# Moving a background task along the kernel, and PSUM copies to ScalarE for a while

## The chip, the cores and the metric

The kernel runs on one core of one Trainium2 chip. The metric is device time in microseconds of one execution; the median of three runs is 2852.82 us (2850.33 to 2859.31).

## The reference

One layer of a hybrid decoder, for a prompt of 2048 tokens and, beside it, 8 sequences of 4 new tokens each ("sample", 32 rows) that attend to caches of 2048 tokens. All is float32, the model width is 1024.

```python
h = rms_norm(x, norm_pre_mix)
q, k, v, z1, z2, g_a, g_b = project_inputs(h, w_in, b_gate)   # one matmul 1024 x 5376, gelu on z, sigmoid on g
for gi, (win, dil) in enumerate(((128, 1), (512, 4), (2048, 16))):   # three head groups, dilated windows
    o, lse = dilated_group_prompt(...)  or  dilated_group_sample(..., cache)
o_a = merge_dilations(outs, lses)                 # weighted by softmax of the lse
o_b = z1 * (tril(w_spatial) @ layer_norm(z2) + b) # gMLP, chunks of 128 tokens
merged = g_a * (o_a @ w_ao) + g_b * (o_b @ w_bo)
x = x + rms_norm(merged @ w_out, norm_post_mix)
f = square(relu(rms_norm(x, norm_pre_ffn) @ w_up)) @ w_down   # 1024 -> 4096 -> 1024
x = x + rms_norm(f, norm_post_ffn)
```

The outputs are the prompt's and the sample's rows, the new keys and values of each group, and the sample's normalised gate rows.

## The kernel before

**Spans.** The prompt is worked in two spans of 1024 tokens; the 32 sample rows ride with span 0, whose rows count 1056. Every matmul operand is split into a high and a low float32r part (`split`, `split_w`, `in_parts`: a cast on ScalarE, then a subtraction on VectorE or GpSimd), and a product takes three matmuls. `gemm` (matmuls at L323) adds them up in a PSUM bank of 512 columns.

**Stages.** For each span: projections of q, k and v with attention behind them (`project`, `attention`: two pairs of heads times three groups), then the gMLP (`gmlp`), then the gates and the merge. In span 0 that is `mix(0)`, eight blocks m of gates, o_a @ w_ao and o_b @ w_bo; in span 1 it is `mix_seven`, which takes the gates of m = 1 to 7 by Strassen's scheme: seven products of quarter matrices (L1236) instead of eight. `out_rows` multiplies by w_out, norms and adds. Then `ffn`: `up(0)` and `down(0)` for span 0, `up(1)` and `down_rows` for span 1, all by the same seven products (matmuls at L1599 and L1707), each over 16 blocks u in `up`. In `up(0)` a product is 4 x 3 x 2 matmuls of 264 columns.

**Weight sums.** The seven products need sums of the quarters of a weight matrix beside the quarters: S1 to S4, for the gates (`gate_sums`), for w_up (`up_sums`) and for w_down (`down_sums`). `weight_sums` makes them in DRAM by DMAs alone, in 20 groups: 4 for the gates, 8 for w_up, 8 for w_down. For each of a group's four sums a plain copy of 512 KB goes out on SyncE's queue (L1454), and one group later an accumulating DMA on GpSimd's queue (L1459) adds the second term. Each of these 160 DMAs is one step of a generator. S2 of a group waits for its S1, S4 for its S2.

**Lanes.** Four deques of generators (`lanes`) hold work that is woven into the main program. `step(lane)` runs the next piece of the first generator in a lane; `tick` steps lanes 0 to 2 at set places inside a product. Lane 0 has attention, gMLP and norm pieces, lane 1 merges and staging, lane 2 sample attention (`sample_attention(0)` and `(1)`, whose VectorE products read the caches piece by piece), one block of the gMLP's gate, `sample_branch` and the next span's first norms (`pre_mix_behind`). Lane 3 has only the weight sums.

**The pacer.** Lane 3 is stepped by columns. `pace(columns)` is called at the start of each `gemm` with the number of k blocks times the columns, and at each of the 49 products of `mix_seven` with 4 x 512:

```python
calls = [-200000]
def pace(columns):
    calls[0] += columns
    if calls[0] > SUM_EVERY:
        calls[0] -= SUM_EVERY
        step(3)
```

So the steps begin after 200,000 columns, in span 0's gMLP, and what is left of them when `mix_seven` is done is drained in one go at the start of `ffn`. `SUM_EVERY` is 3600. The sizes of the calls: 8 x 352 in span 0's projections, gMLP and gates, 2 and 4 times 352 (320 once) in its merge products; 8 x 512 in span 1's projections and gMLP and in the first four products of `mix_seven`; then 2 x 512 and 4 x 512 by turns in 32 merge products; then the 49.

**Copies.** `copy_any` moves a PSUM bank to SBUF, by turns on ScalarE (L196) and VectorE (L198). It is used in `attention` (v transposed, the transposed probabilities, the values' products), in `gmlp` (z2), in `mix_seven` (the merge products) and in `out_rows`.

**Order.** Within each engine the instructions run in one order, chosen when the program is built by a planner with a simulated timeline; pieces of lanes 1 and 2 are held behind what PE, VectorE, ScalarE and GpSimd were given before, pieces of lane 3 behind what GpSimd was given before, and a step's copy behind the last weight load. VectorE, ScalarE, GpSimd and SyncE's queue wait in that order.

**Lines that the prediction names.** L303: the low part of a weight on GpSimd. L350 and L351: the two halves of `split`. L709 to L711: scores on PE and their mask and minimum on VectorE. L920, L957: sample attention's products. L1130: the sums of `forms` in `mix_seven`, with their stores to `gt`. L1179: VectorE's gate product in `mix_seven`, m = 0. L1243 and L1246: evacuation of a gate product and its sigmoid. L1254: the multiplication with `pbx`, loaded from `pb`. L1290 and L1292: gate products in `mix(0)`. L1509 and L1510: the halves of a weight in `weight_stream`, on ScalarE and GpSimd.

Of the kernel before, what the change touches and what calls it, by code (L numbers as in the profile page):

```python
# [40 lines left out]
C_ID, C_STD, C_RES, C_ONE, C_BD, C_REP, C_SMP = 0, 128, 384, 640, 648, 680, 712  # L41
C_ALL = 832

SUM_EVERY = 3600

# [65 lines left out]
def hybrid_step(ctx: ExitStack, tc: tile.TileContext, ins: dict, outs: list):  # L113
# [77 lines left out]
    flip = [0]  # L191

    def copy_any(out, in_):
        flip[0] ^= 1
        if flip[0]:
            nc.scalar.copy(out, in_)  # L196
        else:
            nc.vector.tensor_copy(out, in_)  # L198
# [6 lines left out]
    lanes = [deque(), deque(), deque(), deque()]  # L205

    def push(lane, gen):
        lanes[lane].append(gen)
        return gen

    @contextmanager
    def in_order(*engines):

        left = set(engines)
        with ExitStack() as held:
            for ins in reversed(list(nc.cur_bb.bb.instructions)):
                if not left:
                    break
                if ins.engine in left:
                    left.discard(ins.engine)  # L220
                    held.enter_context(tc.issue_after(ins))
            yield

    def step(lane):
        while lanes[lane]:
            try:
                with in_order(*ORDERED[lane]):
                    next(lanes[lane][0])
                return True
            except StopIteration:  # L230
                lanes[lane].popleft()
        return False

    def tick(some=(0, 1, 2)):
        for lane in some:
            step(lane)

    def drain(lane, gen=None):

        while (lanes[lane] if gen is None else gen in lanes[lane]) and step(lane):  # L240
            pass
# [62 lines left out]
        return wh, wl  # L304


    calls = [-200000]

    def pace(columns):
        calls[0] += columns  # L310
        if calls[0] > SUM_EVERY:
            calls[0] -= SUM_EVERY
            step(3)

    def gemm(w, offs, rhs, n, ticks=SLOW, kind="g"):

        pace(len(offs) * n)
        pt = bank(kind)
        last = len(offs) - 1
        for i, o in enumerate(offs):  # L320
            xh, xl = rhs(i)
            for j, (a, b) in enumerate(((w[0], xh), (w[0], xl), (w[1], xh))):
                nc.tensor.matmul(  # L323
                    pt[:, :n], a[:, o : o + P], b, start=(i == 0 and j == 0), stop=(i == last and j == 2)
                )
            tick(ticks.get(i, ()))
        return pt[:, :n]
# [313 lines left out]
    def attention(s, hp, g, idx, q, v):  # L641
# [14 lines left out]
        for hf in range(2):  # L656
            pt = ps.tile([P, 512], F32, tag="t", name="pt")
            for j in range(4):
                u = hf * 4 + j
                nc.tensor.transpose(pt[:, j * P : (j + 1) * P], v[:, u * P : (u + 1) * P], ident)  # L660
            copy_any(vt[:, hf * 4 : hf * 4 + 4, :], pt.rearrange("p (u c) -> p u c", u=4))
            yield
# [73 lines left out]
        def transposed(u):  # L736
            nk = 2 if prev_of(u) else 1
            w = nk * P
            pb = probs.pop(u)
            pt = ps.tile([P, 2, 2 * P], F32, tag="t", name="pt")  # L740
            for h in range(2):
                for e in range(nk):
                    nc.tensor.transpose(pt[:, h, e * P : (e + 1) * P], pb[:, h, e * P : (e + 1) * P], ident)  # L743
            tb = ring("t", A_T, 512, 2).rearrange("p (h k) -> p h k", h=2)
            copy_any(tb[:, :, :w], pt[:, :, :w])
            trans[u] = tb
# [370 lines left out]


    def mix_seven():
        order = [4, 5, 6, 7, 0, 1, 2, 3]  # L1120
        lo, hi = slice(0, 512), slice(512, HALF)
        halves = (lo, hi)
# [93 lines left out]
        for n, (m, i) in enumerate(seq):  # L1216
# [13 lines left out]
            X = {X11: a[:, lo], X12: a[:, hi], X21: b[:, lo], X22: b[:, hi]}  # L1230
            w, x = next(ws), ops[SEVEN[p][1]]
            pace(4 * 512)
            pt = bank("g")
            for k in range(4):
# [240 lines left out]
    def differ(b11, b12, b21, b22, t1, v, t4):  # L1475

        nc.vector.tensor_tensor(t1, b11, b12, ALU.subtract)
        nc.vector.tensor_tensor(b12, b22, b12, ALU.subtract)
        nc.vector.scalar_tensor_tensor(v, t1, -1.0, b22, ALU.mult, ALU.subtract)
        nc.vector.scalar_tensor_tensor(t4, v, -1.0, b21, ALU.mult, ALU.subtract)  # L1480
        return t1, v, b12, t4
# [8 lines left out]
    def up_form(form, f):  # L1490

        if form in SUMS:
            src = up_d[SUMS.index(form), :, f * P : (f + 1) * P]
        else:
            i, j = int(form[1]) - 1, int(form[2]) - 1
            src = ins["w_up"][0][j * 512 : j * 512 + 512, i * 2048 + f * P : i * 2048 + (f + 1) * P]
        return src.rearrange("(k p) m -> p k m", p=P)
# [14 lines left out]
    def weight_stream(srcs):  # L1512

        for i in range(0, len(srcs), 2):
            two = srcs[i : i + 2]
            raw, _ = fetch_w(two)
            for j, src in enumerate(two):
                nk = src.shape[1]
                t = wp.tile([P, 2, 512], F32R, tag=("wh", "wl")[j], name="wf")
                in_parts(t[:, 0], t[:, 1], raw[:, j * 512 : (j + 1) * 512], nc.gpsimd)  # L1520
                yield t.rearrange("p a (k m) -> p a k m", k=nk)


    def ffn():
# [56 lines left out]
        def product_bank(s):  # L1581
            if s == 0:
                return po[0].tile([P, 1024], F32, tag="d", name="pd")
            return po[0].tile([P, 512], F32, tag="e", name="pe", bufs=6)
# [7 lines left out]
        def result(s, pt):  # L1592
            return pt[:, 248 : 248 + two] if s == 0 else pt

        def mults(s, pt, w, x, first, last):

            for j, (a, b) in enumerate(((0, 0), (0, 1), (1, 0))):
                for c, n, o in pieces(s):
                    nc.tensor.matmul(  # L1599
                        pt[:, o : o + n], w[:, a], x[:, b, c : c + n], start=first and j == 0, stop=last and j == 2  # L1600
                    )

        def gather(res, uses, X):
            for to, add in uses:
                if add is None:
                    nc.scalar.copy(X[to], res)
                else:
                    nc.vector.tensor_tensor(X[to], res, X[add], ALU.add)  # L1608

        def up(s, ops):  # L1610
            n = HALF_T[s]
            at = {X11: 0, X21: 1, X22: 2, X12: 5}
            blks = [[ov[:, o + i * n : o + (i + 1) * n] for i in range(7)] for o in (0, 7 * n)]
            order = [(u, p) for u in range(16) for p in range(7)]
            if s == 0:

                order[:14] = [(u, p) for p in range(7) for u in range(2)]
            ws = weight_stream([up_form(SEVEN[p][0], u) for u, p in order])
            for u, p in order:
                _, b, uses = SEVEN[p]  # L1620
                blk = blks[u % 2]
                X = {x: blk[i] for x, i in at.items()}
                w = next(ws)
                x = ops[b]
                pt = product_bank(s)
                for k in range(4):
                    mults(s, pt, w[:, :, k], x[k], k == 0, k == 3)
                    if k in (1, 3):
                        tick()
                gather(result(s, pt), uses, X)  # L1630
                for q in ((), (), (), (X22,), (X11,), (X21,), (X12,))[p]:
                    nc.scalar.activation(X[q], X[q], AF.Relu, scale=1.0 if q in (X11, X12) else -1.0)
                    nc.scalar.square(X[q], X[q])
                o = u % 2 * 7 * n
                if p == 5:
                    nc.sync.dma_start(f_d[s][u, :, 0:3], ov[:, o : o + 3 * n].rearrange("p (i c) -> p i c", i=3))
                if p == 6:
                    differ(X[X11], X[X12], X[X21], X[X22], blk[3], blk[4], blk[6])
                    nc.sync.dma_start(
                        f_d[s][u, :, 3:7], ov[:, o + 3 * n : o + 7 * n].rearrange("p (i c) -> p i c", i=4)  # L1640
                    )
# [159 lines left out]
        def prepare(s, names, which):  # L1801
            return {b: fill(name, HALF_T[s], h2_form(s, b)) for name, b in zip(names, which)}

        while lanes[3]:
            step(3)
        ops = {}

        def behind(b):
# [9 lines left out]
        ops.update(prepare(0, ("s2",), forms[6:]))  # L1818
        for gen in later:
            push(1, gen)  # L1820
        up(0, ops)
        drain(0)
        drain(1)
        ops1 = {}
        gain_last = {}

# [46 lines left out]
    for s in range(2):  # L1873
# [25 lines left out]
        if s == 0:  # L1899
            mix(0)  # L1900
            early = out_rows(0)
        else:
            mix_seven()
    ffn()
    pools[0].__exit__(None, None, None)

# [43 lines left out]
```

## Time and profile before

| | |
|---|---|
| median of three runs | 2852.82 us |
| profiled execution: own time | 2853.56 us |
| its span in the trace | 2851.9 us |
| TensorE busy | 2805.7 us, 98% |
| VectorE, ScalarE, GpSimd busy | 48%, 45%, 47% |
| mean share of the DMA engines in the copies' queue q1 and the accumulates' queue q0 | 55.0%, 8.7% |
| mean granted TensorE clock | 0.998 |

Times in the rows are microseconds from the start of the span. A row of the windows gives a stretch, its length, for each engine the busy time and the number of instructions, then the granted clock of TensorE, the share of the 16 DMA engines that was busy and the GB/s that they moved. A row of the waits gives who waited at which line for whom, the total in us, how often and the longest. A row of the groups gives line, engine, operation, tiles and shapes, the count, the busy time in us and the mean in ns, then the idle time before them. Matmuls are pipelined, so their single durations overlap; the time of a chain of them, divided by the count, is their rate.

### The profile page before, as it was taken

The numbers are of one execution on the slowest core, as the hardware profiler recorded it, in microseconds if no ns is written. First come the engines' busy times: TensorE is split into PE (matmuls) and PEld (weight loads), VectorE is DVE, ScalarE is ACT, GpSimd is POOL, SyncE is SP. The second block draws the span as 40 slices with busy tenths as digits, with TensorE's granted clock in tenths as the row PEclk, the third lists the DMA queues.
The fourth block names the chain that finished last, engine by engine and source line by source line (L and its number), as shares of the span: only waits on it lengthen the run. The fifth ranks groups of instructions, "written<-read, shape, count | busy, mean of one in ns | idle before, by whom it ended". The sixth has DMA issues, their size and how long they took to land.

```text
span 2851.9 us, 45811 instructions
## 1 busy us (share of the span) xinstructions
PE 2805.7 (98%) x17350; PEld 2551.3 (89%) x17350; DVE 1375.0 (48%) x2318; ACT 1288.6 (45%) x2519; POOL 1329.6 (47%) x1167
## 2 busy tenths in 40 slices
PE   8999999999999999999999999999999999999998
PEld 8999999999988888877888999999999888888887
DVE  4557464752544434554555546442424644452225
ACT  5444452213654444433346544453434544554334
POOL 3346434564123444444761444455546644445553
PEclk9999999999999999999999999999999999999999
DMA  4344345875677665499867878676656766586665
GB/s 140 104 126 136 93 126 162 221 203 152 206 196 217 167 157 150 121 221 271 227 177 253 278 233 297 197 257 194 214 177 218 235 202 193 185 283 195 190 188 169
DMA packets 486606, 550.95 MB, mean 193 GB/s; under 512 B 28273, under 2 KB 373425, under 8 KB 476658
## 3 DMA queue, kind: packets, MB, share of 16 engines
q1 hardware_dynamic: 472992, 502.60, 55.0%
q0 software_dynamic: 13248, 45.36, 8.7%
q8 instruction: 137, 2.24, 0.3%
q14 instruction: 83, 0.68, 0.1%
q10 hardware_dynamic: 146, 0.07, 0.0%
HBM read 425.54 MB, written 206.27 MB: 222 GB/s over the span
## 4 chain that ended last, share of the span: by engine, by line
PE 84%; DVE 6%; DMA 5%; ACT 2%; issue 2%; POOL 1%; SPq 0%; DVEq 0%; POOLq 0%; ACTq 0%
PE pg L323 25%; PE pd L1599 22%; PE pe L1599 11%; PE pe L1707 10%; PE pg L337 5%; PE pg L1236 2%; PE pu L757 2%; PE pt L743 1%; DMA gbc<-in_cache_kv_w_dram 1%; PE ps L323 1%; PE ps L709 1%; DMA raw<-in_w_in_dram 1%; PE ps L710 1%; POOL wf L1510 1%; PE pt L366 1%
## 5 line engine op out<-in xcount | busy, mean ns | idle before, releaser
L1510 POOL TENSOR_TENSOR wf<-raw,wf 128x512 fp32r<-128x512 f32 x493 | 699.8, 1426 | 725.8 <-ACT wf L1509 688.3
L323 PE MATMUL pg<-act,wh 128*128 128x352 f32 (+2 forms) x2976 | 796.4, 346 | 2.4 <-DVE xt L1292 1.4
L323 PEld LDWEIGHTS pg<-act,wh 128*128 128x128 f32 x2976 | 522.3, 189 | 32.5 <-DVE xt L1292 1.7
L1509 ACT CAST wf<-raw 128x512 fp32r<-128x512 f32 x493 | 304.7, 619 | 531.0 <-PE pd L1599 182.8
L323 PE MATMUL pg<-act,wl 128*128 128x352 f32 (+3 forms) x1488 | 512.5, 345 | 0.0
L303 POOL TENSOR_TENSOR wl<-raw,wh 128x512 fp32r<-128x512 f32 (+1 forms) x184 | 242.2, 1345 | 300.9 <-ACT wh L299 262.5
L1599 PE MATMUL pd<-act,wf 128*128 128x264 f32 x2880 | 361.2, 285 | 1.3 <-ACT ov L196 1.0
L1599 PEld LDWEIGHTS pd<-act,wf 128*128 128x128 f32 x2880 | 354.0, 189 | 2.0 <-ACT ov L196 1.4
L323 PEld LDWEIGHTS pg<-act,wl 128*128 128x128 f32 x1488 | 280.2, 188 | 17.1
L1707 PE MATMUL pe<-wf,act 128*128 128x512 f32 (+1 forms) x984 | 224.3, 389 | 1.4 <-ACT wf L1509 1.2
L1707 PEld LDWEIGHTS pe<-wf,act 128*128 128x128 f32 x984 | 181.7, 188 | 43.1 <-ACT wf L1509 1.4
L1608 DVE TENSOR_TENSOR ov<-pd,ov 128x528 f32<-128x528 f32 x140 | 96.2, 704 | 193.4 <-PE pd L1599 188.2
L1599 PE MATMUL pd<-pair,wf 128*128 128x264 f32 x1440 | 183.2, 284 | 0.0
L1599 PE MATMUL pe<-act,wf 128*128 128x512 f32 x768 | 182.6, 392 | 0.1
L1510 DVE TENSOR_TENSOR act<-flat,act 128x1024 fp32r<-128x1024 f32 (+1 forms) x76 | 102.1, 1346 | 162.4 <-ACT act L1509 162.4
L1599 PEld LDWEIGHTS pd<-pair,wf 128*128 128x128 f32 x1440 | 177.9, 188 | 0.0
L1599 PEld LDWEIGHTS pe<-act,wf 128*128 128x128 f32 x768 | 143.8, 188 | 32.9 <-ACT pair L1509 0.3
L299 ACT CAST wh<-raw 128x1024 fp32r<-128x1024 f32 (+1 forms) x91 | 91.7, 1009 | 173.3 <-PE pg L323 94.3
L1608 DVE TENSOR_TENSOR ov<-pe,ov 128x512 f32<-128x512 f32 x136 | 91.5, 687 | 137.3 <-PE pe L1599 126.4
L1599 PE MATMUL pd<-oa,wf 128*128 128x264 f32 x1056 | 135.0, 284 | 0.0
L715 ACT ACTIVATE ov<-ov 128x256 f32<-128x256 f32 (+1 forms) x192 | 91.8, 478 | 92.9 <-DVE ov L711 90.4
L1599 PEld LDWEIGHTS pd<-oa,wf 128*128 128x128 f32 x1056 | 130.8, 188 | 0.0
(340 smaller groups left out, 4619.4 us busy)
## 6 DMA issues: line engine op xcount, KB each, us to landing
raw<-in_w_in_dram SPq DMA_DIRECT2D x70, 512.0 KB
raw<-up_sums SPq DMA_DIRECT2D x128, 256.0 KB
raw<-down_sums SPq DMA_DIRECT2D x128, 256.0 KB
flat<-f SPq DMA_DIRECT2D x48, 528.0 KB
raw<-in_w_up_dram SPq DMA_DIRECT2D x96, 256.0 KB
raw<-in_w_down_dram SPq DMA_DIRECT2D x96, 256.0 KB
flat<-f SPq DMA_DIRECT2D x48, 512.0 KB
f<-ov SPq DMA_DIRECT2D x16, 1056.0 KB
```

The source lines that it names most:

```text
L299: nc.scalar.copy(wh[:, :o], raw[:, :o])
L303: eng.tensor_tensor(wl[:, c], raw[:, c], wh[:, c].bitcast(F32), ALU.subtract)
L323: nc.tensor.matmul(pt[:, :n], a[:, o : o + P], b, start=(i == 0 and j == 0), stop=(i == last and j == 2))
L337: nc.tensor.matmul(pt[:n, o : o + width], a, b, start=(i == 0 and j == 0), stop=(i == last and j == 2))
L715: nc.scalar.activation(pb[:, h, :w], pb[:, h, :w], AF.Exp, scale=-1.0, bias=stats[:, u, h : h + 1], accum_out=stats[:, u, 2 + h : 3 + h],)
L757: nc.tensor.matmul(up[:, hs], tb[:, h, e * P : (e + 1) * P], vv[:, hs], start=(e == 0), stop=(e == len(rows) - 1),)
L1236: nc.tensor.matmul(pt, w[:, c, k], x[k][:, d], start=k == 0 and j == 0, stop=k == 3 and j == 2)
L1509: nc.scalar.copy(high, raw)
L1510: eng.tensor_tensor(low, raw, high.bitcast(F32), ALU.subtract)
L1599: nc.tensor.matmul(pt[:, o : o + n], w[:, a], x[:, b, c : c + n], start=first and j == 0, stop=last and j == 2)
L1608: nc.vector.tensor_tensor(X[to], res, X[add], ALU.add)
L1707: nc.tensor.matmul(pts[i][:, cs], x[k][:, c, t * P : (t + 1) * P], w[:, d, 0, cs], start=k == 0 and j == 0, stop=k == 15 and j == 2,)
```

## The change

Four things are changed. `copy_any` uses ScalarE whenever lane 2 holds anything, and alternates only otherwise. `SUM_EVERY` becomes 2800. A flag is set when `mix_seven` begins and taken back before `up(0)`; while it is set, `pace` adds no columns (its test against `SUM_EVERY` and the step behind it are made as before). `up` calls `pace` once per product, with 4 x 528 x 3 // 7 = 905 columns in `up(0)`. The drain of lane 3 at the start of `ffn` is moved behind `up(0)`.

```diff
-SUM_EVERY = 3600
+SUM_EVERY = 2800
...
     def copy_any(out, in_):
         flip[0] ^= 1
-        if flip[0]:
+        if flip[0] or lanes[2]:
             nc.scalar.copy(out, in_)
         else:
             nc.vector.tensor_copy(out, in_)
...
+    held_back = [False]
     calls = [-200000]
 
     def pace(columns):
-        calls[0] += columns
+        if not held_back[0]:
+            calls[0] += columns
         if calls[0] > SUM_EVERY:
             calls[0] -= SUM_EVERY
             step(3)
...
     def mix_seven():
+        held_back[0] = True
...
                 x = ops[b]
+
+                pace(4 * n * 3 // 7)
                 pt = product_bank(s)
...
-        while lanes[3]:
-            step(3)
         ops = {}
...
+        held_back[0] = False
         up(0, ops)
-        drain(0)
-        drain(1)
+        for lane in (0, 1, 3):
+            drain(lane)
```

## The prediction

> **What bounds the kernel now.** I read the busy shares first, then the windows by stage, then the PE's waits in the two stretches where it idles.
>
> ```profile
> span 2851.9 us, 45811 instructions
> PE 2805.7 (98%) x17350; PEld 2551.3 (89%) x17350; DVE 1375.0 (48%) x2318; ACT 1288.6 (45%) x2519; POOL 1329.6 (47%) x1167
> ```
>
> TensorE is busy in 2805.7 of 2851.9 us. An edit that removes no matmul can win at most the 46.2 us of idle time, and whatever a lowered clock costs. So the question is where those microseconds lie. The windows (length, busy time and count of each engine, granted clock, share of the DMA engines, GB/s):
>
> ```profile
> 80.00:330.00 250.00, 246.64 (x1697) 239.55 (x1696) 158.83 (x425) 117.15 (x333) 121.69 (x145) 1.00 0.42 120
> 440.00:606.00 166.00, 161.55 (x1005) 160.19 (x1004) 105.97 (x147) 39.08 (x64) 86.44 (x74) 1.00 0.77 206
> 700.00:815.00 115.00, 114.90 (x785) 103.85 (x784) 67.21 (x105) 65.28 (x179) 21.65 (x19) 1.00 0.59 200
> 1225.00:1290.00 65.00, 61.02 (x253) 48.07 (x252) 37.99 (x58) 21.70 (x31) 27.91 (x32) 0.95 0.93 243
> 1290.00:1460.00 170.00, 160.66 (x690) 129.62 (x690) 98.99 (x119) 70.84 (x120) 102.79 (x85) 0.99 0.88 237
> 1257.70:1264.50 6.80, 5.20 (x12) 3.62 (x13) 6.80 (x5) 0.00 (x0) 6.75 (x7) 0.50 0.97 213
> 1264.50:1310.00 45.50, 45.13 (x195) 36.24 (x195) 23.47 (x31) 12.86 (x22) 15.54 (x14) 1.00 1.03 303
> 1455.70:1459.10 3.40, 3.40 (x10) 2.62 (x9) 3.21 (x5) 2.06 (x4) 1.28 (x1) 0.50 0.02 7
> 1550.00:1650.00 100.00, 99.55 (x819) 99.16 (x820) 56.68 (x74) 54.40 (x98) 46.83 (x34) 1.00 0.88 286
> ```
>
> The second span's gates (mix_seven) fill about 1225 to 1460. They hold 3.98 + 9.34 = 13.3 us of the idle time, and twice the clock is granted at half (6.8 and 3.4 us), which costs up to half of that time, 5.1 us. Span 0's attention (80 to 330) idles 3.36 us, its second sample attention (440 to 606) 4.45, the start of the feed-forward 0.45. What PE waited for in the gates, first up to 1290, then from there:
>
> ```profile
> PE pg L323 <- POOL wl L303: 1.7, 1, 1.7
> PE ps L323 <- DVE xt L1179: 1.6, 1, 1.6
> PE pg L1236 <- DVE xt L1243: 7.2, 3, 2.8
> PE pg L1236 <- DVE gx L1243: 2.2, 1, 2.2
> ```
>
> And what kept POOL, ScalarE and VectorE late (timeline; in brackets the idle time before the instruction and what ended it):
>
> ```profile
> 1255.72 0.78 POOL L1459 DMA_DIRECT2D down_sums<-down_sums  x1 [5.86 <-DMA gt<-junk]
> 1327.06 0.62 ACT L350 CAST pair<-gt 128x512 fp32r<-128x512 f32 x1 [3.80 <-DMA gt<-gt]
> 1346.90 0.69 DVE L1254 TENSOR_TENSOR xt<-xt,pbx 128x512 f32<-128x512 f32 x1 [4.58 <-DMA pbx<-pb]
> 1443.19 5.18 DVE L351 TENSOR_TENSOR act<-ov,act 128x512 fp32r<-128x512 f32 x4
> 1449.12 3.01 PE L1236 MATMUL pg<-act,wf 128*128 128x512 f32 x12 [1.58 <-DVE xt L1243]
> 1454.90 1.38 PE L1236 MATMUL pg<-oa,wf 128*128 128x512 f32 x4 [2.77 <-DVE xt L1243]
> ```
>
> There are three groups. Near 1255 POOL stood 5.86 us at an accumulating step and everything behind it came late. Near 1331 and 1348 (2.8 and 2.2 us) the evacuation queued behind data that arrived late by DMA. Near 1449 and 1455 (1.58 and 2.77 us) the evacuation queued behind four splits on VectorE, which wait for no DMA.
>
> **The change part by part.** *Where the 160 steps of the weight sums go.* Twenty groups give four copies and four accumulates each. A call of the pacer adds its columns and lets out at most one step. Before, the threshold is 3600; counting call by call gives 5 steps in the first gMLP, 51 in mix(0), 36 in the second span's projections, 16 in its gMLP, 52 in mix_seven. After, at 2800: 6, 67, 36, 16, 24 and 11 in up(0). The projections and the gMLP there call with 8 x 512 = 4096 columns, so they let out one step a call under either threshold and the surplus piles up: 52 x (4096 - 2800) = 67,000 columns, 24 steps. The hold stops only the adding; the test against the threshold stays. So the first 24 calls of mix_seven still let out one step each, and the pause begins behind them. The rows for its length and for prices:
>
> ```profile
> 1312.26 16.52 PE pg L1236 x72
> 1619.82 2.92 PE pd L1599 x24
> q1 hardware_dynamic: 472992, 502.60, 55.0%
> q0 software_dynamic: 13248, 45.36, 8.7%
> L1454 SPq DMA_DIRECT2D down_sums<-in_w_down_dram x10: 496/578/1975, 1302.6 to 1400.6; - x10
> L1459 POOL DMA_DIRECT2D down_sums<-down_sums x10: 764/780/800, 1290.9 to 1438.5; - x10
> L1459 POOL DMA_DIRECT2D down_sums<-in_w_down_dram x8: 855/875/977, 1298.3 to 1421.8; - x8
> ```
>
> A 512-column matmul takes 16.52/72 = 0.229 us, three to a column block, 1.34 ns per paced column. The 24 calls hold 4 x 4096 and 10 x (1024 + 2048) columns, 47,100, or 63 us: the burst ends near 1290. Before, the same calls let out about 20 steps. A step's DMA time: the accumulates' queue took 0.087 x 2851.9 = 248 us for 45.36 MB, 2.87 us for 0.524 MB; the copies' queue 0.55 x 2851.9 us for 502.6 MB, 1.64 us.
>
> *mix_seven to 1290:* 20 steps become 24, DMA stays near its ceiling. The 3.98 us of idle and up to 3.4 of lowered clock stay: 0. Bounds: -6.5 if POOL no longer stands (a residue of 0.9 stays), +4 if the four more steps delay as the others did (20 steps went with 3.98).
>
> The clock fell at 1257.7 about the waits of 1.7 and 1.6 us. The Trainium skill, "TensorE: Matmul & The Clock Gate", Part 1, says that the array drops to half rate after an idle window of about 3.4 us; no single wait here is that long, so the trace differs unless short waits add up within a window. By the rule as written, removing these short waits would not return the 3.4 us, and the -6.5 would be -3.1; the sum below, which takes 0 here, is the same by both.
>
> *mix_seven from 1290:* the 10 copies and 18 accumulates go, 10 x 1.64 + 18 x 2.87 = 68 us of 170, so the share falls from 0.88 to 0.48, and SP and POOL each lose these issues (0.58 and 0.8 to 0.9 us apiece) ahead of weight loads and subtractions. The gt and pbx loads then land sooner; next late is the sigmoid on ScalarE, which I leave 0.7 us. -2.8 - 2.2 + 0.7 = -4.3. Bounds: 0, and -10.4 if the last pair (4.35 us) and its half clock (up to 1.7) go too. I take -4.3: the splits near 1443 depend on row sums and POOL, not on loads.
>
> *Copies.* Lane 2 holds sample attention from about 82 to 325, so what alternated goes to ScalarE:
>
> ```profile
> L198 DVE COPY ov<-pu x40: 273/292/293, 90.8 to 316.3; 128x128 f32<-128x128 f32 x40
> L198 DVE COPY ov<-pt x6: 683/688/692, 82.7 to 329.6; 128x512 f32<-128x512 f32 x6
> PE ps L709 <- DVE ov L711: 3.2, 7, 0.9
> L196 ACT COPY ov<-pu 128x128 f32<-128x128 f32 x48 | 12.5, 261 | 44.4 <-PE pu L757 44.1
> L196 ACT COPY ov<-pt 128x512 f32<-128x512 f32 x39 | 22.7, 582 | 27.9 <-PE pt L660 10.3 <-PE pu L757 9.9 <-PE pt L743 7.4
> ```
>
> VectorE loses 40 x 0.292 + 6 x 0.688 = 15.8 of 158.8 busy us; ScalarE gains 40 x 0.261 + 6 x 0.582 = 13.9 on 117 of 250. PE's waits here are 3.2 us on VectorE's masked scores, which queue behind sample attention and these copies. I take -1.5. Bounds: -3.2 (all go), +1.5 (as much lost to queueing behind ScalarE's exponentials). In out_rows(0) about 11 copies move because lane 2 holds other work; PE is busy 114.90 of 115 there, three banks cover it: 0. If that cover went, 11 x 0.58 = 6.4 us is the most.
>
> *mix(0).* In 440 to 606 the 17 copies of the next two rows, with as many accumulates, grow by 3600/2800 to 44 steps, some 10 more at a mean of 2.25 us: 22 us of DMA, share 0.77 to 0.90. Sample attention's cache loads go through it, and VectorE waits for them in order, the gate products behind it:
>
> ```profile
> L1454 SPq DMA_DIRECT2D gate_sums<-in_w_in_dram x8: 513/592/1093, 452.2 to 521.3; - x8
> L1454 SPq DMA_DIRECT2D up_sums<-in_w_up_dram x9: 505/581/1497, 523.1 to 602.9; - x9
> PE ps L323 <- DVE xt L1290: 2.2, 1, 2.2
> DVE prod L920 <- DMA gbc<-in_cache_kv_w_dram: 9.5, 2, 7.8
> ACT wf L1509 <- PE pd L1599: 16.4, 11, 2.8
> ACT wf L1509 <- DMA raw<-in_w_up_dram: 5.8, 2, 3.9
> ```
>
> The nearest row in share is 1290:1460 at 0.88: without its last pair 5.0 us idle in 170, 4.9 in 166, +0.4 over today's 4.45. The row at 0.93 (3.98 idle and 3.4 clock in 65) gives 18.8 in 166, +14.4. I take +2, near the first. Lower bound -1, as today's waits may fall elsewhere.
>
> *up(0).* 11 steps, 3 copies and 8 accumulates, one in 2800/905 = 3.1 products of 2.92 us, 9 us: 1550 to 1650. They add 3 x 1.64 + 8 x 2.87 = 27.9 us of DMA to 88 in 100: 16 too many, and up to 1.4 us of POOL ahead of a weight's subtraction. ScalarE's casts waited for PE 11 times and for weights twice (the last two rows), so weights run ahead. Window 1264.5:1310 shows a share of 1.03 with 0.37 us idle in 45.5: +0.8 in 100. I take +1.5; bounds 0 and +16.
>
> The Trainium skill, "DMA: Bandwidth & Descriptors", section "Issuing engines are not separate DMA queues", says that DMAs of all issuers run on the same 16 engines and interleave; no run so far shows which transfer suffers in up(0). If it is the weight loads, the price is the +16 of the third rival.
>
> **Sum.** 0 - 4.3 - 1.5 + 2 + 1.5 = -2.3 us on this execution, whose own time is 2853.56 (1.66 around the span), 0.74 above the median of 2852.82: 2851.3 here, 2850.5 as a median. A measurement tells about 0.3%, 8.6 us, from no change.
>
> **The rivals.**
> *The pause frees all the gates.* The early group goes too, because POOL meets its step with the transfer already landed (the steps are 17 further on). For: it was one wait of 5.86 us. Against: the burst keeps its rate. -2.3 - 6.5 = -8.8, with the copies' full -3.2 it is -10.5: 2842.3.
> *mix(0) pays the early price.* Saturated as 1225 to 1290 is: +14.4 instead of +2, net +10.1: 2862.9; half of it stays within 0.3%. Against: 1264.5:1310.
> *up(0) starves (the other sign).* The 16 us too many reach PE through late weights: -2.3 + 14.5 = +12.2: 2865. It is slower by over 0.3% from 12.4 of the 16 on. Against: weights run ahead there.
> *The hold does nothing that counts.* The gates' waits are VectorE's own order: the 4.3 stay, +2: 2854.8.
>
> **How the numbers follow.** Forecast 0.40 (0.04 of it faster by over 0.3%, when the last pair goes too); everything freed 0.28 (all faster); mix(0) 0.10 (half slower); up(0) 0.14 (slower); nothing 0.08 (same). Faster 0.32, same 0.36 + 0.05 + 0.08 = 0.49, slower 0.19. The range takes in the freed gates with the copies' bound, 2842.3 less one for the median's spread, and stops at 2861, which leaves out most of the up(0) and some of the mix(0) case; the forecast's own range is 2844 to 2856.
>
> **What would show it.** Right: steps of L1454 and L1459 in 1225 to 1290 as dense as before, none to 1460, a share near 0.5 from 1290; waits near 1331 and 1348 gone, the pair before 1460 and one half-clock stretch near 1258 still there; 40 copies of pu gone from VectorE before 330; 11 steps in 1550 to 1650 with PE idle under 3 us. Wrong: no half-clock stretch in the gates; PE idle over 10 us in 440 to 606 or 1550 to 1650.

## The result, and the profile after

The changed kernel takes 2863.83 us (median of six runs, 2861.44 to 2868.71) against 2852.99 us for the kernel before (six runs, 2850.33 to 2859.31): a ratio of 1.0034, interval 1.0023 to 1.0045. It is about 11 us slower; 2850.5 was forecast, and the range ended at 2861. The profiled execution of the changed kernel is the slowest of its six (2868.71 us), so its terms below are to be set against the 15.1 us between the two spans (2867.0 and 2851.9), not against 11. One execution of a later kernel (the slower pace) took 9795.92 us; it is in no ratio and in no profile.

The page of the changed kernel, its span and its busy shares:

```profile
span 2867.0 us, 45819 instructions
PE 2811.3 (98%) x17350; PEld 2558.8 (89%) x17350; DVE 1357.5 (47%) x2264; ACT 1303.4 (45%) x2573; POOL 1328.2 (46%) x1167
```

The 15.1 us of span are 55.7 - 46.2 = 9.5 us more idle time of TensorE and 5.6 us more busy time for the same 17350 matmuls; the half-clock stretches below are more than enough for that. The windows say where. First the rows of the kernel before that the prediction doesn't show (length, busy time and count of PE, PEld, DVE, ACT and POOL, granted clock, DMA share, GB/s):

```profile
820.00:1240.00 420.00, 418.56 (x2387) 361.82 (x2386) 177.62 (x472) 190.98 (x449) 187.41 (x238) 1.00 0.65 168
1240.00:1300.00 60.00, 56.02 (x230) 43.90 (x229) 40.06 (x51) 14.91 (x25) 25.18 (x26) 0.94 0.98 267
1300.00:1475.00 175.00, 165.66 (x774) 136.54 (x773) 99.84 (x116) 74.25 (x123) 111.52 (x89) 0.99 0.84 228
1560.00:1670.00 110.00, 109.65 (x906) 109.26 (x905) 58.58 (x79) 54.75 (x95) 51.44 (x37) 1.00 0.85 276
```

Then the same columns for the kernel after; the last five rows are its half-clock stretches:

```profile
80.00:330.00 250.00, 245.30 (x1699) 240.72 (x1697) 147.65 (x383) 128.02 (x379) 120.52 (x143) 0.99 0.42 122
440.00:606.00 166.00, 156.38 (x964) 155.23 (x963) 99.23 (x136) 40.16 (x65) 88.47 (x77) 0.98 0.86 228
820.00:1240.00 420.00, 417.16 (x2382) 358.52 (x2381) 180.71 (x471) 190.55 (x456) 183.75 (x232) 1.00 0.65 166
1240.00:1300.00 60.00, 51.49 (x215) 40.61 (x214) 31.31 (x50) 17.05 (x25) 25.47 (x29) 0.93 0.94 231
1300.00:1475.00 175.00, 174.75 (x801) 143.98 (x800) 102.70 (x129) 79.03 (x128) 98.79 (x75) 1.00 0.51 157
1560.00:1670.00 110.00, 104.07 (x835) 103.31 (x834) 59.36 (x75) 52.38 (x92) 48.99 (x41) 0.97 0.99 298
267.30:270.70 3.40, 3.40 (x15) 3.33 (x14) 2.33 (x5) 0.59 (x1) 0.92 (x1) 0.50 0.96 261
543.80:547.20 3.40, 3.40 (x14) 3.40 (x13) 0.54 (x3) 3.29 (x4) 0.65 (x1) 0.50 1.11 284
601.80:612.00 10.20, 5.80 (x20) 5.81 (x21) 6.95 (x11) 0.53 (x1) 3.64 (x4) 0.50 0.79 227
1291.30:1301.50 10.20, 5.55 (x13) 4.44 (x14) 6.56 (x9) 2.53 (x4) 1.96 (x2) 0.50 1.00 336
1615.60:1622.40 6.80, 5.89 (x27) 5.92 (x28) 3.99 (x7) 0.84 (x2) 0.78 (x1) 0.50 1.06 278
```

Length less PE's busy time is its idle time; half of the busy time in a half-clock stretch is at most what the clock cost. By stage, idle before and after:

| stage | idle before | idle after | clock, more or less | total |
|---|---|---|---|---|
| span 0's attention, 80 to 330 | 3.36 | 4.70 | +1.7 | +3.0 |
| mix(0), 440 to 606 (to 612 for the clock) | 4.45 | 9.62 | 1.7 + 2.9 | +9.8 |
| span 1's projections, 820 to 1240 | 1.44 | 2.84 | 0 | +1.4 |
| early gates, 1240 to 1300 | 3.98 | 8.51 | 2.8 - 2.6 | +4.7 |
| the rest of the gates, 1300 to 1475 | 9.34 | 0.25 | -1.7 | -10.8 |
| up(0), 1560 to 1670 | 0.35 | 5.93 | +2.9 | +8.5 |

They add up to 16.6, 1.5 above the 15.1 of the two spans. The idle columns give 8.9 of the 9.5 us; the clock column gives 7.7 where TensorE's busy time grew by 5.6, so half of the busy time is about a quarter too much there. The pause wins 10.8 us where it holds; three other stages pay 23. The steps went nearly where the count in the prediction put them. The rows of the sums (the two lines that issue them, count, ns of one, from when to when) in the three windows 1240:1300, 1300:1475 (none) and 1560:1670 of the kernel after; an eleventh step for up(0), a copy, goes out ahead of the stage, at 1492.8:

```profile
L1457 SPq DMA_DIRECT2D down_sums<-in_w_down_dram x5: 497/509/877, 1241.5 to 1271.7; - x5
L1462 POOL DMA_DIRECT2D down_sums<-in_w_down_dram x5: 863/881/1191, 1240.5 to 1282.5; - x5
L1462 POOL DMA_DIRECT2D down_sums<-down_sums x5: 770/803/1047, 1243.1 to 1278.5; - x5
...
L1457 SPq DMA_DIRECT2D down_sums<-in_w_down_dram x2: 563/715/867, 1567.4 to 1585.5; - x2
L1462 POOL DMA_DIRECT2D down_sums<-down_sums x5: 771/781/787, 1584.2 to 1658.1; - x5
L1462 POOL DMA_DIRECT2D down_sums<-in_w_down_dram x3: 870/877/877, 1566.1 to 1627.2; - x3
```

What TensorE waited for in the three stages that pay, and what kept the engine late for which it waited (timeline of the kernel after; in brackets the idle time and its releaser):

```profile
605.02 0.69 DVE L959 TENSOR_TENSOR prod<-ov,zs 128x512 f32<-128x512 f32 x1 [6.77 <-DMA ov<-in_cache_kv_w_dram]
606.20 0.90 PE L325 MATMUL ps<-oa,wh 128*128 128x320 f32 x2 [7.21 <-DVE xt L1293]
1294.07 1.23 DVE L1133 TENSOR_TENSOR junk<-act 128x1024 f32<-128x1024 f32 x1 [12.73 <-DMA gt<-junk]
1295.95 1.22 PE L325 MATMUL ps<-oa,wh 128*128 128x512 f32 x2 [7.91 <-DVE ov L198]
1612.31 1.36 ACT L1512 CAST wf<-raw 128x512 fp32r<-128x512 f32 x2 [5.38 <-DMA raw<-up_sums]
1615.65 0.71 DVE L1611 TENSOR_TENSOR ov<-pd,ov 128x528 f32<-128x528 f32 x1 [6.59 <-DMA f<-ov]
1616.51 5.84 PE L1602 MATMUL pd<-act,wf 128*128 128x264 f32 x25 [3.74 <-DVE ov L1611]
```

The three have one form. VectorE takes its instructions in order. The next one stands for a DMA: a cache load in mix(0), the store of `junk` that must have left before `junk` is written again in the gates, the store of `ov` in up(0). The evacuation of the PSUM bank stands behind it (in up(0) it is the evacuation itself that waits, as it writes `ov`), and TensorE behind that. In up(0) the weights were late as well (5.38 us), but the wait of 3.74 us ended on the store.

The form isn't new. In mix(0) of the kernel before, VectorE stood 3.12 us for such a load with the evacuation L1292 next, and TensorE waited 1.4 us for that:

```profile
600.27 0.92 DVE L957 TENSOR_TENSOR prod<-gbc,zs 128x512 f32<-128x512 f32 x1 [3.12 <-DMA gbc<-in_cache_kv_w_dram]
```

The planner also chose a new order. With the new pace alone some 18 of VectorE's 2321 instructions stand elsewhere, all of them in mix(0), near 1030 and in the gates. No run has the new steps in the old order, so what the order adds to the loss stays open.

### The profile page after: what moved, and what is told of

It reads as the page before. It is cut to its first block, busy times and chain, and to the rows that moved or that the text cites. A ratio compares the mean times of both kernels' runs of the same rounds, so it can differ in the third digit from the quotient of the medians.

```text
span 2867.0 us, 45819 instructions
## 1 busy us (share of the span) xinstructions
PE 2811.3 (98%) x17350; PEld 2558.8 (89%) x17350; DVE 1357.5 (47%) x2264; ACT 1303.4 (45%) x2573; POOL 1328.2 (46%) x1167
## 4 chain that ended last, share of the span: by engine, by line
PE 83%; DVE 7%; DMA 6%; issue 2%; ACT 2%; POOL 1%; SPq 1%; DVEq 0%; POOLq 0%; ACTq 0%
PE pg L325 25%; PE pd L1602 19%; PE pe L1602 11%; PE pe L1712 9%; PE pg L339 7%; PE pg L1239 4%; PE pu L759 2%; PE ps L325 1%; PE pt L745 1%; DMA xt<-h 1%; PE ps L711 1%; DMA us<-ov 1%; PE ps L712 1%; DMA gt<-junk 1%; DMA junk<-us 1%
## 5 line engine op out<-in xcount | busy, mean ns | idle before, releaser
L1512 ACT CAST wf<-raw 128x512 fp32r<-128x512 f32 x493 | 304.7, 619 | 547.4 <-PE pd L1602 172.1
L1611 DVE TENSOR_TENSOR ov<-pd,ov 128x528 f32<-128x528 f32 x140 | 96.1, 704 | 201.1 <-PE pd L1602 192.6
L1611 DVE TENSOR_TENSOR ov<-pe,ov 128x512 f32<-128x512 f32 x136 | 91.5, 688 | 137.1 <-PE pe L1602 126.2
L713 DVE CUSTOM_DVE_ANT_0 ov<-ps,con 128x256 f32<-128x256 f32 (+1 forms) x192 | 72.3, 384 | 140.5 <-PE ps L712 133.0
```

The costliest lines, as they stand in the source:

```text
L713: nc.vector.tensor_tensor_reduce(pb[:, h, :w], sp[:, h, :w], mask[:, 2 * P - w : 2 * P], 1.0, 3.0e38, ALU.add, ALU.min, stats[:, u, h : h ...
L1512: nc.scalar.copy(high, raw)
```

## The experiments

The main theory going in, A in the expectations: a step costs by the bytes that it puts on the DMA engines, and only where an engine with TensorE behind it waits in order for a DMA; so places with slack can be found for the steps. Rivals, named as the expectations name them: the copies, or the order that the planner makes of them, cost the time (B); the pace is harmless, and the pause and the calls in `up` cost (B2); the issues on GpSimd's and SyncE's queues cost, not the bytes (C); the early gates' stall doesn't come from the steps issued there (D); the price moves with the steps to wherever they go (C2, E in the later runs).

**The copies alone** (before, with the new condition in `copy_any`):

```diff
-        if flip[0]:
+        if flip[0] or lanes[2]:
```

> The kernel before with only the edit of the copies: ScalarE takes every copy while lane 2 holds work, the weight sums as before. Theory A (the loss of the changed kernel is the DMA time of the weight sums, put where loads are waited for in order): the copies are worth -1.5 us, 2849 to 2854 us; VectorE's 40 copies of the values' products before 330 us are gone, PE's waits for the masked scores fall from 3.2 to about 2 us, and mix(0) idles 4 to 5 us in 440 to 606 as before. Theory B (the copies on ScalarE, or the new order that the planner makes of them, cost the time): 2858 us or more, with PE idle over 8 us in 440 to 606.

Measured: 2856.34 against 2855.51 us, 1.0005 (0.9995 to 1.0015). Its waits of PE in 80:330:

```profile
PE pt L619 <- DVE smp L584: 2.7, 1, 2.7
PE ps L709 <- DVE ov L711: 2.5, 3, 1.2
```

The wait at the scores fell from 3.2 to 2.5 us, and a new one of 2.7 stands beside it. The stage idles 5.2 us instead of 3.4, and mix(0) 5.2 instead of 4.5. The copies gain nothing, so A's 2849 to 2854 is missed; but they don't bring the loss either, as B had it.

**The sums alone** (after, with the alternating copies):

```diff
-        if flip[0] or lanes[2]:
+        if flip[0]:
```

> The changed kernel with the copies put back to taking turns, all edits of the weight sums kept. Theory A: 2860 to 2868 us, as the changed kernel, with the same three places: 440 to 606, 1240 to 1300 and 1560 to 1670, each with PE idle over 4 us. Theory B: 2848 to 2855 us.

Measured: 2863.32 us, 1.0024 (1.0015 to 1.0033). The windows of its three paying stages:

```profile
440.00:606.00 166.00, 156.77 (x968) 155.70 (x967) 102.89 (x140) 38.02 (x62) 86.22 (x75) 0.98 0.85 228
1240.00:1300.00 60.00, 51.04 (x211) 40.24 (x210) 31.99 (x46) 16.12 (x24) 23.05 (x25) 0.91 0.96 241
1560.00:1670.00 110.00, 104.44 (x838) 103.68 (x837) 58.41 (x74) 53.91 (x93) 51.78 (x43) 0.97 0.96 291
```

They idle 9.2, 9.0 and 5.6 us, nearly as in the whole change. The loss comes with the edits of the sums.

**The same issues with fewer bytes** (after; each accumulating DMA adds the first eighth of its rows, so seven eighths of the sums' second terms are left out):

```diff
-nc.gpsimd.dma_start(todo[j][i][0], todo[j][i][2], accum_op=ALU.add, ...)
+r = todo[j][i][0].shape[0] // 8
+nc.gpsimd.dma_start(todo[j][i][0][:r], todo[j][i][2][:r], accum_op=ALU.add, ...)
```

> The changed kernel, but each accumulating DMA of the weight sums adds only the first eighth of its rows; every DMA is still issued, waited for and counted. Theory A (bytes on the DMA engines): an accumulate's 2.87 us of DMA fall to about 0.4, the idle time of PE falls from 9.6 to under 5 us in 440 to 606, from 8.5 to under 3 in 1240 to 1300 and from 5.9 to under 2.5 in 1560 to 1670, the half-clock stretches with them: 2836 to 2846 us. Theory C (the steps cost by their issue, on GpSimd and on SyncE's queue, ahead of weights and loads): 2858 to 2867 us.

Measured: 2847.43 us, 0.9973 (0.9961 to 0.9985), 16.4 us below the whole change, and 1.4 above the range that A gave. The windows, and the wait in mix(0) that was 6.77 us in the whole change:

```profile
440.00:606.00 166.00, 161.84 (x995) 160.88 (x994) 111.66 (x149) 39.94 (x65) 93.79 (x81) 0.98 0.61 184
1240.00:1300.00 60.00, 56.15 (x241) 44.35 (x240) 41.31 (x51) 16.01 (x26) 23.03 (x26) 1.00 0.64 200
1560.00:1670.00 110.00, 107.67 (x891) 107.27 (x890) 54.77 (x76) 54.80 (x91) 53.40 (x44) 1.00 0.84 269
595.54 0.97 DVE L959 TENSOR_TENSOR prod<-ov,zs 128x512 f32<-128x512 f32 x1 [3.46 <-DMA ov<-in_cache_kv_w_dram]
```

With every issue in its place, the idle time falls to 4.2, 3.9 and 2.3 us. So most of the price is the accumulates' bytes, and C, which had 2858 us or more, falls as the main cause. Not all goes: in up(0) 2.0 us more than before remain, and in the early gates 3.1 us more than without any step (0.79 us, next run). Whether that is the copies' bytes or the issues, the run doesn't say. It also idles 6.3 us in 2500:2840, against 1.6 in the whole change; the runs don't explain that.

**A pause that stops the steps too** (after; `pace` returns at once while the flag is set):

```diff
-        if not held_back[0]:
-            calls[0] += columns
+        if held_back[0]:
+            return
+        calls[0] += columns
```

> The changed kernel, but the pacer does nothing at all while it is held, so the 24 steps of the surplus go to up(0) too, 35 there instead of 11, one in 3.1 products, 1550 to about 1870 us. Theory A: 1240 to 1300 idles under 2 us instead of 8.5 at full clock, worth -8 to -12 with the half clock; 440 to 606 as in the changed kernel; up(0) costs what it cost in its first 100 us and 1 to 6 us more behind them: 2852 to 2862 us. Theory D (the stall at 1287 is VectorE's own order of the forms and their stores): 1240 to 1300 still idles over 5 us, 2862 us or more.

Measured: 2884.40 us, 1.0101 (1.0086 to 1.0117).

```profile
1240.00:1300.00 60.00, 59.21 (x256) 47.17 (x255) 40.60 (x56) 18.02 (x29) 21.36 (x20) 1.00 0.47 157
1560.00:1670.00 110.00, 90.03 (x662) 87.41 (x661) 53.75 (x59) 38.62 (x62) 41.95 (x38) 0.89 1.05 306
```

Without the burst the early gates idle 0.79 us at the full clock, so the steps do cause that stall, and D falls. The counter's surplus was kept, however, and in up(0) a call adds 905 columns where a step takes 2800: the 33 steps left came out one per product in all but one case, issued from 1475.2 to 1679.4. At a DMA share of 1.05 up(0) idles 20.0 us to 1670. The expectation had 35 steps, spread out; that was my error in reading the counter. It shows what a dense burst costs there.

**The pace alone** (before, with `SUM_EVERY = 2800`):

```diff
-SUM_EVERY = 3600
+SUM_EVERY = 2800
```

> The kernel before with one number changed: a step in 2800 columns instead of 3600. 6, 67, 36, 16 and then 35 steps in mix_seven, one at each of its first calls, none in up(0). Theory A (DMA time where loads are waited for in order): 440 to 606 idles about 9 us as in the changed kernel and 1240 to 1300 at least 6, up(0) at most 0.5, 1300 to 1475 about half of its 9.3 us: 2856 to 2866 us. Theory B2 (the faster pace itself is harmless, the hold and the new calls in up cost the time): 440 to 606 idles 4 to 5 us, 2850 to 2857 us.

Measured: 2861.79 against 2854.96 us, 1.0027 (1.0016 to 1.0039).

```profile
440.00:606.00 166.00, 156.58 (x964) 155.51 (x963) 103.13 (x142) 37.91 (x62) 86.00 (x74) 0.97 0.85 228
1240.00:1300.00 60.00, 49.13 (x208) 38.58 (x207) 27.58 (x40) 13.64 (x20) 23.23 (x25) 0.92 0.98 241
```

The constant alone brings the price of mix(0) (9.4 us idle) and of the early gates (10.9).

**Later steps in up(0)** (after; `pace` is called in `up` from block 6 on):

```diff
-                pace(4 * n * 3 // 7)
+                if u >= 6:
+                    pace(4 * n * 3 // 7)
```

> The changed kernel, but up(0) calls the pacer only from block u = 6 on, so that its 11 steps fall behind 1680 us, where the DMA engines are busy 0.74 of the time instead of 0.85. Theory A: 1560 to 1670 idles under 1 us at full clock instead of 5.9, the stretch of the moved steps under 2: 2852 to 2859 us. Theory C2 (a step in up(0) costs TensorE time wherever it stands, by its issue on GpSimd ahead of the weights): the 5.9 us and the half clock move with the steps, 2860 us or more.

Measured: 2863.12 us, 1.0027 (1.0015 to 1.0039). Its windows, and a row of the waits in 1670:1900 (total us, times, longest):

```profile
1560.00:1670.00 110.00, 108.82 (x901) 108.61 (x900) 58.41 (x80) 55.04 (x95) 50.26 (x37) 1.00 0.85 275
1670.00:1900.00 230.00, 224.55 (x1834) 223.78 (x1833) 117.53 (x144) 109.24 (x178) 106.08 (x83) 0.99 0.82 256
```

```profile
ACT wf L1512 <- DMA raw<-up_sums: 32.4, 10, 9.8
```

In the whole change the two windows idle 5.93 and 0.52 us, here 1.18 and 5.45: 6.45 and 6.63. The price moved with the steps, as C2 had it, and A's 2852 to 2859 failed. It came mostly through late weights (PE waited 3.2 us for casts of them at L1512 and 1.9 for VectorE's L1611), and ScalarE's casts stood for the weights' DMA, not for GpSimd's issues, which C2 had named. A free place in up(0) was not found.

**A slower pace from the start** (before; the steps begin at once, every 6000 columns to the end of the first gMLP, 4600 in mix(0), 2500 in span 1, and no surplus is kept):

```diff
-    calls = [-200000]
+    calls = [0]
+    every = [6000]      # 4600 from mix(0) on, 2500 from span 1 on
...
-        if calls[0] > SUM_EVERY:
-            calls[0] -= SUM_EVERY
+        while calls[0] > every[0]:
+            calls[0] -= every[0]
```

> The kernel before with the 160 steps spread by stage so that none is left for mix_seven or up(0): from the first column on, one step in 6000 columns to the end of the first gMLP, one in 4600 in mix(0), one in 2500 in the second span up to its gMLP's end, several in a call where a call is longer. Copies take turns as before. Theory A: 440 to 606 idles under 4 us (40 steps in mix(0) instead of 51), 1225 to 1475 under 2 at full clock, up(0) as before, 820 to 1240 under 4 at a DMA share near 0.85: 2834 to 2844 us. Theory E (the steps cost about the same wherever they are put, TensorE loses the same time elsewhere): 2850 to 2857 us.

Measured: 2858.30 us, 1.0017 (1.0006 to 1.0029).

```profile
80.00:330.00 250.00, 237.87 (x1622) 231.96 (x1622) 160.36 (x413) 112.95 (x318) 125.39 (x148) 0.99 0.56 157
820.00:1240.00 420.00, 413.54 (x2362) 355.85 (x2361) 178.42 (x472) 188.90 (x461) 191.51 (x243) 0.99 0.76 195
```

mix(0) to 606 and the early gates are freed (0.61 and 0.78 us idle), and the attention and the projections pay: 12.13 us instead of 3.36, and 6.46 instead of 1.44; 606 to 700 idles 4.2 instead of 0.2. This is E's outcome, not A's 2834 to 2844. In the projections VectorE stood for one small load (timeline of the same kernel):

```profile
848.17 1.21 DVE L1363 TENSOR_TENSOR flat<-flat 32x1024 f32<-32x1024 f32 x1 [13.30 <-DMA flat<-in_x_sample_dram]
```

**No surplus at the pause, and later steps in up(0)** (after; a call lets out as many steps as are due, and up(0) begins at block 6):

```diff
-        if calls[0] > SUM_EVERY:
+        while calls[0] > SUM_EVERY:
...
+                if u >= 6:
+                    pace(4 * n * 3 // 7)
```

> The changed kernel, but the pacer lets out as many steps in a call as are due, so no surplus is left when it is held (149 steps before mix_seven, none in it), and up(0) calls it only from block u = 6 on. Theory A: 1240 to 1300 and 1560 to 1670 each idle under 1.5 us at full clock, 440 to 606 stays at 9 to 10 with its half clock, 820 to 1240 at 3 to 5: 2842 to 2850 us. Theory E: 2855 us or more, with the idle time in 820 to 1240.

Measured: 2854.95 us, 1.0001 (0.9990 to 1.0013).

```profile
440.00:606.00 166.00, 154.57 (x938) 152.96 (x937) 103.49 (x140) 37.87 (x62) 85.03 (x74) 0.97 0.84 227
820.00:1240.00 420.00, 416.39 (x2375) 359.00 (x2374) 180.97 (x472) 189.30 (x451) 191.51 (x243) 1.00 0.71 184
1670.00:1900.00 230.00, 226.01 (x1847) 225.41 (x1846) 117.70 (x142) 108.54 (x177) 105.80 (x83) 0.99 0.84 266
```

All the gates are free, and mix(0) (11.4 us idle), the projections (3.6) and up(0) (2.0 to 1670 and 4.0 behind it, before 0.4) give it all back: the 2855 of E, not the gain of A.

**The steps into span 1's projections** (before; 3600 until span 1's second projection group, index 7, then 1900, no surplus; so no step is left for the gates or for up(0)):

```diff
+    every = [3600]
...
                 if idx == 7:
                     new_slot(3, False)
+                    every[0] = 1900
```

> The kernel before with a step in 3600 columns up to the second span's first projection, then one in 1900, several in a call, so that all 160 are out before mix_seven; copies take turns. Nothing is added in span 0's attention, in mix(0) or in up(0). Theory A (a step costs TensorE time only where loads are waited for in order by an engine that TensorE needs soon): 1225 to 1475 idles under 2 us at full clock (before 13.3 and 10.2 us at half clock), 820 to 1240 under 4 us at a DMA share near 0.8, the rest as before: 2838 to 2846 us. Theory E (the steps cost about the same wherever they stand): 2850 to 2857 us, with over 10 us of idle time in 820 to 1240.

Measured: 2848.97 against 2854.13 us, 0.9989 (0.9978 to 1.0000).

```profile
820.00:1240.00 420.00, 411.86 (x2341) 354.81 (x2340) 174.09 (x463) 185.25 (x442) 202.80 (x257) 1.00 0.85 218
1240.00:1300.00 60.00, 59.21 (x257) 47.26 (x256) 40.73 (x60) 19.66 (x29) 20.28 (x20) 1.00 0.47 157
595.50:598.90 3.40, 3.09 (x11) 3.09 (x12) 0.40 (x2) 0.00 (x0) 3.40 (x3) 0.50 1.08 390
711.60:715.00 3.40, 3.40 (x18) 3.40 (x18) 2.03 (x3) 1.84 (x3) 3.15 (x4) 0.50 0.57 163
1035.80:1039.20 3.40, 3.40 (x17) 3.21 (x17) 1.24 (x5) 2.70 (x8) 2.66 (x3) 0.50 0.47 139
```

Of 13.3 us of idle time in the gates 1.0 is left, and the projections idle 8.1 instead of 1.4. With the clock's 4.3 that would be 9.9 us won; the profiled executions differ by 4.6. The idle time of all the rest is about as before: in all it fell from 46.2 to 40.3 us, by 5.9, and gates and projections make 5.6 of that. What is lost again is clock: the last three rows are half-clock stretches that the kernel before doesn't have, at most 4.9 us. The first comes with a wait of 2.87 us, the third behind one of 2.77, and the second with no wait at all. The expectation of 2838 to 2846 missed by its size. This is the best version found, and its interval reaches 1.

**Steps in `out_rows` and its kin too** (the same, with 2150, and `pace(1800)` at the start of `gemm_rows`):

```diff
+        pace(1800)
         pt = bank("g")
```

> As the run before, but the first span's output rows (700 to 820 us, DMA share 0.6, PE not idle) take 12 of the steps too, and the second span's projections one in 2150 columns. Theory A: 700 to 820 stays under 1 us idle, 820 to 1240 a little under the other kernel: 2837 to 2846 us. Theory E: 2850 us or more, with idle time in 700 to 860, where the next span's rows and norms are loaded.

Measured: 2854.97 us, 1.0006 (0.9997 to 1.0015).

```profile
700.00:820.00 120.00, 117.19 (x787) 105.65 (x786) 64.15 (x102) 64.25 (x176) 27.90 (x26) 0.99 0.75 239
```

This stage idles 2.8 us, where it idled 0.1 in the kernel before, and the DMA share there is no more than 0.75. Here too the outcome is E's, not A's 2837 to 2846.

## Why the prediction was wrong

**The count of the steps** was nearly right: 22 early in the gates instead of 24, none from there to 1475, 11 in up(0). In the true pause, which paces alike up to the gates, 127 steps are out by 1215.1 and 33 come from 1475.2 on; 33 less the 11 of up(0) leaves 22. The prediction counted 36 steps in span 1's projections; the first group calls eight times, four of them with 2048 columns, so they are 38. The same count gives 51 instead of 52 in the gates of the kernel before, where the first 22 calls let out 19.

**mix_seven to 1290, taken as 0 with a bound of +4: failed.** It is +4.7. I argued that a share near its ceiling can't rise, so nothing changes. The share stayed (0.98 and 0.94), but one store of a buffer landed later, and VectorE's wait of 12.73 us made one stall of 7.9. Idle rose by 4.5 us. The share says how busy the DMA engines are, not for which transfer an engine stands in line.

**mix_seven from 1290, taken as -4.3:** mechanism right, size off, -10.8 measured, 0.4 beyond the bound. The last pair of waits (1.58 + 2.77 us and half a clock stretch) went too. I had put it down to the order of VectorE's splits, because these waited for no DMA themselves. With the steps gone the pair was gone; which of the transfers had made the splits late, the runs don't show.

**mix(0), taken as +2: failed.** +9.8. I took the price from the row nearest in share (0.88, 5 us in 170); the second rival took it from the early gates (+14.4). The choice between the two rows was wrong: what decides is what stands in line. In mix(0) VectorE stood 6.77 us for a cache load with TensorE's evacuation right behind it, as in the early gates (12.73 us); in the row that I chose the waits for DMAs were 3.80 and 4.58 us. The lowered clock, of which I had put nothing into this term, is 4.6 of the 9.8.

**up(0), taken as +1.5 with a bound of +16: failed by size.** +8.5. "Weights run ahead" was read from ScalarE's casts in the kernel before, and stores were left out of it: the longest wait ended on the store `f<-ov`. The Trainium skill, "DMA: Bandwidth & Descriptors", section "Issuing engines are not separate DMA queues", says that DMAs of every issuing engine interleave on the same 16 engines. The traces agree: thinning the accumulates of GpSimd's queue alone, with the same issues, took up(0)'s idle time from 5.9 to 2.3 us.

**The copies, taken as -1.5:** 40 copies left VectorE before 330, and the kernel with them alone is 1.0005 (0.9995 to 1.0015), so about nothing. In 80 to 330 the two profiled executions with the copies idle 4.7 and 5.2 us instead of 3.4 and have a half-clock stretch of 3.4 us each; the term had put nothing there for the new wait of 2.7 us.

**The rivals.** Each had one stage pay, as one mechanism against the rest. mix(0) and up(0) paid together, each a part of its price, because one cause is behind both: the steps' bytes, ahead of a load or a store that VectorE stands for. Chances worked out as if one case excluded the others left out the case that came.

**The clock.** In the early gates the half clock goes with the short waits: in the true pause, the slower pace and the kernel with the steps moved ahead, 1240:1300 idles 0.78 to 0.79 us at a clock of 1.00. So the full -6.5 was the bound, and the -3.1 worked out by the idle window of the Trainium skill's "TensorE: Matmul & The Clock Gate", Part 1, was not. What the Trainium skill says there of the window's length fits the stretches: each is 3.4 us or two to four times that, but for the one that ends each kernel. What led to them doesn't: a single wait of 2.02 us was enough for one, and some came with no wait (last section). Short waits don't always bring one either: in the thinned run 3.85 us of them (1.60 the longest) remain in 1240:1300 at a clock of 1.00.

**What stays open:** why the price of a step differs as it does: 0.8 us in up(0) (8.5 for 11 steps), 0.6 in mix(0) (9.8 for 16 more), 0.3 in the gates of before (12.3 us of idle time and 4.3 of clock for 51), 0.16 in span 1's projections and gMLP of the best version (6.7 of idle time and at most 1.7 of clock for the same 51, not counting that version's half-clock stretches elsewhere). And how much of it is the planner's order.

## What to carry to other kernels

A background transfer on shared DMA engines is not hidden because TensorE looks busy or the share is below 1: look for the in-order engine that stands for a load, or for a store that frees a buffer, with TensorE's evacuation next in its queue, and price the transfer there. Before moving such work out of a stage that stalls, price the place that it goes to by the same question, and add the places up, since they pay together. A counter that is stopped but still tested goes on working off its surplus: count the calls, not the intent.

## What the runs showed of the hardware

- TensorE's clock fell to half behind single waits of 2.02 us (3.4 us of half clock at 543.8) and 2.67 us (3.4 at 267.3), 3.74 (6.8), 7.21 and 7.91 (10.2 each) in the kernel after. Apart from the stretch that ends each kernel, all lengths are multiples of 3.4 us; the longest is 13.65 (the true pause and the pace alone). Waits of 2.8 and 2.2 us in the gates of the kernel before brought none.
- It also fell with no wait. 32 matmuls of 32 columns stand in `sample_branch`, 30 of them in 3.59 us at 708.4 in the best version, and 3.4 us of half clock follow at 711.6. Four of the twelve profiled executions have such a stretch behind them, the others, the kernels before and after among them, have none.
- A load of 128 KB (`flat`, 32 x 1024) kept VectorE idle for 13.30 us in a stretch with a mean DMA share of 0.76.
- The share alone tells little: 1.03 with 0.4 us idle in 45.5 (before, 1264.5:1310), 0.86 with 9.6 us idle in 166 (after, mix(0)), 0.75 with 2.8 us idle in 120 (the last kernel).
